# Laying out the rows of three tiles in sixteen shared sections of 1.5 MB, in an instance norm that is bound by DMA

## The chip, the cores and the metric

The kernel runs on one core of a Trainium2 chip. The metric is device time in microseconds of one execution. A ratio in this text is the mean time of one kernel's fast runs over that of the other's fast runs of the same rounds, so it is not quite the ratio of the medians that are quoted beside it.

Some terms: HBM is the memory that holds the input and the output (the page counts 1073.74 MB read from it and as many written), SBUF the memory of the core that holds the tiles, used here as 128 partitions. Sixteen DMA engines copy between them in packets; here a packet is mostly the 64 KB of one partition (32,384 of 37,298 packets in the kernel before). VectorE and ScalarE compute (busy 3298.0 and 2407.7 us there), SyncE issues the copies, and each engine waits for the others by semaphores. The trace has 4144 completions for 259 copies, sixteen for each copy, taken here as one from each DMA engine; a copy has landed with its last completion.

## The reference

```python
# x: (256, 256, 4096) float32, drawn from a normal distribution; eps = 1e-5
mean = np.mean(x, axis=2, keepdims=True)
var = np.var(x, axis=2, keepdims=True)
return ((x - mean) / np.sqrt(var + eps)).astype(np.float32)
```

That is 65,536 independent rows of 16 KB. Each row must be read once and written once, 1073.74 MB each way, and it does not matter which rows are worked on together. The change makes use of that freedom.

## The kernel before

A tile is 512 rows: 128 SBUF partitions with K = 4 adjoining rows each, so one partition's part is 64 KB without a gap. There are 128 tiles of 8 MB and three tile buffers. SyncE issues all loads and stores; VectorE sums the rows and normalizes most of them, ScalarE squares and sums and normalizes the rest.

```python
P, K, BUFS = 128, 4, 3
x_t = x_flat.rearrange("(t p k) d -> t p k d", p=P, k=K)      # tile t, partition p, row k
out_t = out_flat.rearrange("(t p k) d -> t p k d", p=P, k=K)
...
def store(s, t):
    take(S, done[s], K + 1)                    # wait for VectorE and ScalarE
    S.dma_start(out=rows_of(out_t, t), in_=X[s][:, :, :]).then_inc(stored[s], 16)

def load(s, t, wait=True):
    if wait:
        take(S, stored[s], 16)                 # the buffer's last store must have landed
    S.dma_start(out=X[s][:, :, :], in_=rows_of(x_t, t)).then_inc(loaded[s], 16)
...
with S.Fori(0, rounds) as i:                   # the steady state
    for t in range(L0, L0 + BUFS):
        store(t % BUFS, (t, BUFS, rounds, i))
        load((t + 2) % BUFS, (t + 2, BUFS, rounds, i))
```

The first tile is loaded and stored in two halves, and the last one is stored in two. In the built program a load copies from an HBM pattern [128 x 16384] to an SBUF pattern [128 x 16384] (elements of 4 bytes, slowest dimension first).

## Time and profile before

| | before |
|---|---|
| time, median | 4961.8 us (4961.51 to 4986.83) |
| busiest compute engine | VectorE, 66% |
| DMA queue 1, share of 16 engines | 100.0% |
| rate over the span | 433 GB/s |
| pace in steady state | 38.67 us per tile |
| 64 KB packets, median / mean | 2.418 / 2.420 us |

The prediction below shows the page's lines, the waits and the chain. The page's row of rates, one number in GB/s for each fortieth of the span, is this:

```profile
GB/s 422 431 435 433 431 435 433 432 437 432 432 438 432 433 437 432 433 437 432 435 435 432 436 434 431 438 433 431 438 433 432 438 432 433 438 432 433 438 432 405
```

### The profile page before, as it was taken

The page shows a single profiled execution, that of the slowest core. Times are in us where ns is not written, and L with a number is a line of the kernel's source. Part 1 is how long each engine was busy: PE and PEld are TensorE (multiplying, and loading weights), DVE is VectorE, ACT ScalarE, POOL GpSimd, SP SyncE. Part 2 cuts the span into 40 slices and gives each one's busy share as a digit, 9 for nine tenths or more (in the row PEclk, how much of TensorE's full clock was granted, in tenths as well). Part 3 has the DMA queues.
Part 4 walks back from the last instruction along what each step waited for, and adds up shares of the span by engine and source line. Part 5 has one row for each costly group of instructions (what it writes and reads, how often), then busy time and mean ns, then how long its engine had stood idle before and what let it go on. Part 6 is the DMA issues. An engine that isn't in the chain of part 4 may idle for free.

```text
span 4960.2 us, 5938 instructions
## 1 busy us (share of the span) xinstructions
DVE 3298.0 (66%) x2049; ACT 2407.7 (49%) x1412; POOL 0.2 (0%) x4
## 2 busy tenths in 40 slices
DVE  6666666666666666666666666666666666666666
ACT  4455444554445544455445544455444554445544
POOL 0000000000000000000000000000000000000000
DMA  9999999999999999999999999999999999999999
GB/s 422 431 435 433 431 435 433 432 437 432 432 438 432 433 437 432 433 437 432 435 435 432 436 434 431 438 433 431 438 433 432 438 432 433 438 432 433 438 432 405
DMA packets 37298, 2147.52 MB, mean 433 GB/s; under 512 B 4144, under 2 KB 4144, under 8 KB 4144
## 3 DMA queue, kind: packets, MB, share of 16 engines
q1 hardware_dynamic: 37296, 2147.50, 100.0%
q14 instruction: 2, 0.02, 0.0%
HBM read 1073.74 MB, written 1073.74 MB: 433 GB/s over the span
## 4 chain that ended last, share of the span: by engine, by line
DVE 62%; another core or an unknown queue 31%; issue 4%; DMA 2%; ACT 0%; DVEq 0%; ACTq 0%; SPq 0%
DVE x L87 44%; DVE x L112 17%; DMA x<-in_x_dram 1%; DVE nbias L100 1%; DMA out_dram<-x 1%; DVE rstd L98 1%; ACT junk L137 0%; DVEq L68 0%; DVEq L219 0%; ACT L146 0%; ACT std L146 0%; ACTq L68 0%; ACTq L67 0%; SPq L265 0%
## 5 line engine op out<-in xcount | busy, mean ns | idle before, releaser
L87 DVE TENSOR_SCALAR_CACHE_REDUCE x<-x 128x4096 f32<-128x4096 f32 x512 | 2232.3, 4416 | 1580.4 <-DMA x<-in_x_dram 1580.4
L137 ACT ACTIVATE junk<-x,mean 128x4096 f32<-128x4096 f32 x512 | 1883.1, 3678 | 2367.2 <-DVE x L87 2367.2
L112 DVE TENSOR_SCALAR x<-x,rstd,nbias 128x4096 f32<-128x4096 f32 (+1 forms) x512 | 1004.2, 2004 | 33.9 <-DVE nbias L100 29.3
L151 ACT ACTIVATE x<-x,nbias,rstd 128x3072 f32<-128x3072 f32 x130 | 383.2, 2948 | 146.2 <-DVEq L68 146.2
L137 ACT ACTIVATION_READ_ACCUMULATOR junk<-x,mean 128x1 f32 x512 | 95.5, 187 | 0.0
L146 ACT ACTIVATE std<-ss,eps_tile 128x2 f32<-128x2 f32 x256 | 75.6, 295 | 19.1
L98 DVE RECIPROCAL rstd<-std 128x2 f32<-128x2 f32 x256 | 40.7, 159 | 19.4 <-ACT std L146 19.4
L100 DVE SCALAR_TENSOR_TENSOR nbias<-mean,rstd 128x2 f32<-128x2 f32 x256 | 41.1, 161 | 8.9
L87 DVE DVE_READ_ACCUMULATOR x<-x 128x1 f32 x512 | 42.3, 83 | 0.0
L137 ACT ACT_TABLE_LOAD x1 | 1.3, 1283 | 1.2 <-DVE eps_tile L216 1.2
L146 ACT ACT_TABLE_LOAD x1 | 1.3, 1283 | 0.1
L216 DVE MEMSET eps_tile<- 128x1 f32 x1 | 0.1, 59 | 1.0 <-SPq L192 1.0
L251 POOL MEMSET const-bfloat16-1.0<- 128x1 bf16 x1 | 0.1, 101 | 0.0
L251 POOL MEMSET const-uint8-127<- 128x1 uint8 x1 | 0.1, 101 | 0.0
L251 POOL MEMSET const-float32-1.0<- 128x1 f32 x1 | 0.1, 99 | 0.0
L251 POOL MEMSET const-float32-0.0<- 128x1 f32 x1 | 0.1, 98 | 0.2 <-issue 0.2
## 6 DMA issues: line engine op xcount, KB each, us to landing
out_dram<-x SPq DMA_DIRECT2D x4, 4096.0 KB, 19.6
x<-in_x_dram SPq DMA_DIRECT2D x2, 4096.0 KB, 16.7
x<-in_x_dram SPq DMA_DIRECT2D x127, 50.3
out_dram<-x SPq DMA_DIRECT2D x126, 31.5
```

What stands on the lines that cost most here:

```text
L87: V.tensor_scalar(out=x[:, r, :], in0=x[:, r, :], scalar1=1.0 / d, scalar2=None, op0=ALU.mult, op1=ALU.add, accum_out=mean[s][:, r : r + 1 ...
L98: mine(V.reciprocal(out=rstd[s][:, c], in_=std[s][:, c]))
L100: mine(V.scalar_tensor_tensor(out=nbias[s][:, c], in0=mean[s][:, c], scalar=-1.0 / d, in1=rstd[s][:, c], op0=ALU.mult, op1=ALU.mult))
L112: V.tensor_scalar(out=x[:, r, f], in0=x[:, r, f], scalar1=rstd[s][:, c], scalar2=nbias[s][:, c], op0=ALU.mult, op1=ALU.add,).then_inc(dn, 1)
L137: mine(A.activation(out=junk, in_=x[:, r, :], func=AF.Square, bias=mean[s][:, c], scale=-float(d), accum_out=ss[s][:, c]))
L146: A.activation(out=std[s][:, c], in_=ss[s][:, c], func=AF.Sqrt, bias=eps_tile, scale=1.0 / d**3).then_inc(stds, 1)
L151: A.activation(out=x[:, last, :Q], in_=x[:, last, :Q], func=AF.Identity, bias=nbias[s][:, c], scale=rstd[s][:, c]).then_inc(dn, 1)
L216: V.memset(eps_tile, eps / d**2).then_inc(ready, 1)
L251: nc = _bacc.Bacc("TRN2", target_bir_lowering=False, num_devices=1)
```

## The change

The intent is that the DMA engines work farther apart in HBM. Three tiles together take a block of 24 MB, cut into E = 16 sections of 1.5 MB; a tile gets a run of 512 KB (8 partitions) in each section, so its runs lie 1.5 MB apart. The first two tiles stay as they were. Computation, waits and the number of DMAs don't change.

```diff
-    x_t = x_flat.rearrange("(t p k) d -> t p k d", p=P, k=K)
-    out_t = out_flat.rearrange("(t p k) d -> t p k d", p=P, k=K)
     assert ntiles == 128
+    E = 16
+    L0 = ntiles % BUFS
+
+    def by_tiles(ap):
+        groups = ap[L0 * P * K :].rearrange("(i e s j k) d -> s i e j k d", e=E, s=BUFS, k=K, j=P // E)
+        rest = ap[: L0 * P * K].rearrange("(t e j k) d -> t e j k d", e=E, k=K, j=P // E)
+        return groups, rest
+
+    x_t, out_t = by_tiles(x_flat), by_tiles(out_flat)
...
-    def rows_of(ap, t):
-        if isinstance(t, int):
-            return ap[t]
+    def rows_of(tiles, t):
+        groups, rest = tiles
+        if isinstance(t, int):
+            return rest[t] if t < L0 else groups[(t - L0) % BUFS][(t - L0) // BUFS]
         first, period, count, i = t
-        ap = ap[first : first + period * (count - 1) + 1 : period]
-        return ap[bass.ds(i, 1)].rearrange("o p k d -> p (o k) d")
+        assert period == BUFS
+        first -= L0
+        ap = groups[first % BUFS][first // BUFS : first // BUFS + count]
+        return ap[bass.ds(i, 1)].rearrange("o e j k d -> e (o j) k d")
... (the same in the half stores and loads)
```

More of the change, by code (lines that the diff above doesn't have):

```diff
@@ L180, in store_half @@
         take(S, second(done, s, h), half + 1)
-        S.dma_start(out=out_t[t][:, r, :], in_=X[s][:, r, :]).then_inc(second(stored, s, h), 16)
+        S.dma_start(out=rows_of(out_t, t)[:, :, r, :], in_=X[s][:, r, :]).then_inc(second(stored, s, h), 16)
     def halves(tile_fn, s, first):
@@ L189 @@
     rounds = (ntiles - 5) // BUFS
-    L0 = 2
     with tc.tile_critical():
@@ L194 @@
             r = half_of(h)
-            S.dma_start(out=X[0][:, r, :], in_=x_t[0][:, r, :]).then_inc(second(loaded, 0, h), 16)
+            S.dma_start(out=X[0][:, r, :], in_=rows_of(x_t, 0)[:, :, r, :]).then_inc(second(loaded, 0, h), 16)
         load(1, 1, wait=False)
```

## The prediction

> **What bounds the kernel now.** I read the page's busy shares and slices first, then its DMA part, then the table of waits, then the chain of work in the middle of the run, and last the records of single DMA packets in the trace.
>
> ```profile
> DVE 3298.0 (66%) x2049; ACT 2407.7 (49%) x1412; POOL 0.2 (0%) x4
> ...
> DMA  9999999999999999999999999999999999999999
> ...
> DMA packets 37298, 2147.52 MB, mean 433 GB/s; under 512 B 4144, under 2 KB 4144, under 8 KB 4144
> ...
> q1 hardware_dynamic: 37296, 2147.50, 100.0%
> HBM read 1073.74 MB, written 1073.74 MB: 433 GB/s over the span
> ```
>
> No compute engine is over 66% busy; the DMA row is 9 in all forty slices, and the packets of queue 1 fill 100.0% of the time of sixteen engines. The bytes are the least possible (1073.74 MB read once, written once). So the time is bytes divided by the rate of the DMA engines.
>
> ```profile
> DVE x L87 <- DMA x<-in_x_dram: 1580.4, 126, 13.2
> ...
> SPq L68 <- DVE x L112: 4757.1, 130, 38.3
> ```
>
> The columns are total us, number of waits, longest. VectorE waits 126 times for a load, 1580.4 / 126 = 12.5 us each: that is its slack in every tile. SyncE's wait for VectorE is long because it issues early and then has nothing to do, not because the DMA rings are empty.
>
> ```profile
> 2009.18 12.44 another core or an unknown queue
> ...
> 2021.72 17.45 DVE x L87 x8
> ...
> 2047.80 12.49 another core or an unknown queue
> ...
> 2060.39 17.45 DVE x L87 x8
> ```
>
> This is the chain of work in steady state; the columns are start and length in us. The row named "another core or an unknown queue" is the wait for a load. One tile takes 2060.39 - 2021.72 = 38.67 us, in which 16.78 MB move: 434 GB/s.
>
> The packet records say the same of one engine: of 32,384 packets of 64 KB (one partition's four rows) the median is 2.418 us, 27.1 GB/s, and the mean 2.420. All bytes at the median would take 32,768 x 2.418 / 16 = 4952.1 us. The span is 4960.2, so 8.1 us in all are above that, start and end included. Only 373 packets took over 2.43 us, 66.4 us too much between them, or 4.1 us per engine.
>
> [...]
>
> **The change part by part.** Compute: VectorE, ScalarE and SyncE have the same instructions in the same order, the same waits and the same number of DMAs (259). Cost 0. Bytes and packets: a partition still holds four adjoining rows, 64 KB, so there should again be 32,384 packets of 64 KB. Cost 0. The first two tiles keep their places.
>
> Addresses in HBM: neighbouring runs of a tile lie 1.5 MB apart instead of side by side. At best all 373 slow packets go: -4.1 us. The early tiles, with the most of them, are unchanged in part, so I count -2.
>
> Shape: this is what the intent does not mention. The HBM side was [128 x 16384] and is now [16 x 8 x 16384], for 126 loads and 126 stores; the SBUF side stays 128 partitions.[...]
>
> [...]Four rows are 4 x 2.418 = 9.67 us. [...]The slack of 12.5 us per tile allows such a lead.
>
> [...]126 tiles cost another 126 x 38.67 = 4872 us: about 9830.[...]
>
> What in the trace speaks for a quick settling is that engines already drift apart in before. The sixteen completions of a load land within 0.4 us at 13 us, 2.4 us at 220 us, 5.1 us at 570 us, and 7.4 us from 1150 us on. The number of slow packets falls with it, from 51 in the first fortieth of the span to 3 to 6 in those around the middle. [...]one-sided and soon over, a loss of about one full lead.
>
> Sum: 4961.8 - 2 + 9.7 + 3 (the last store ends with its last engine, spread 6.5 us in before, now perhaps 9.7) = 4972.5 us.
>
> **Rivals.** First, nothing happens[...]. For it: the author's intent leaves it out[...]. Time: 4958 to 4963. Second, [...]For it: [...]ten of the sixteen completions still lie within 0.8 us of each other at the end of before[...]. Time: 6000 to 9830. Third, slow settling[...]: 5060 to 6000. Fourth, a gain from HBM spacing:[...] a gain over 2% needs packets under 2.37 us, of which before has none.
>
> **Range and chances.** I give nothing-happens and quick settling 0.58 together, slow settling 0.14, lasting collisions 0.27, faster by over 2% 0.01. The predicted time is that of the likeliest case, 4972 us. The lower end is the floor of 4952.1 less a margin, 4948. The upper end cuts off most of the lasting collisions: 7000.
>
> **What would show it.** The packet part should again have 37,298 packets and 2147.52 MB; more packets would mean that rows were cut, and my account of the shape is wrong. [...]many 64 KB packets take up to 4.8 us, first slices of the GB/s row fall to half, and VectorE's wait for loads grows from 12.5 us. Quick settling shows as one or two low slices and then 433; lasting collisions as an even low row.[...] A span under 4948 would make the whole account wrong.

## More of the kernel before

All runs here have a granted clock of 1.0.

One more view is useful for later, the timeline around the first load of tile 2; its columns are start, length, engine, line, operation, and in brackets the idle time before.

```profile
48.78 0.46 SPq L170 DMA_DIRECT2D x<-in_x_dram  x1
...
82.51 4.42 DVE L87 TENSOR_SCALAR_CACHE_REDUCE x<-x 128x4096 f32<-128x4096 f32 x1 [8.22 <-DMA x<-in_x_dram]
```

The load is issued at 48.78 us, queues behind a store whose last completion comes at 63.26 us, and VectorE can start on it at 82.51 us.

## The result

The changed kernel takes 9084.94 us (median of 4 runs, 9007.18 to 9097.58) against 4961.8 us: a ratio of 1.8265, 95% interval 1.8162 to 1.8369. The result is correct. The predicted 4972 us and the range of 4948 to 7000 us were wrong.

First the page of the changed kernel, the lines that answer to those in the prediction. The row GB/s has one number for each fortieth of the span.

```profile
DVE 3298.2 (37%) x2049; ACT 2407.6 (27%) x1412; POOL 0.2 (0%) x4
...
DMA  9999999999999999999999999999999999999998
GB/s 292 250 245 241 239 238 241 236 237 236 237 238 237 237 235 238 235 238 236 236 236 239 240 238 238 237 238 239 238 235 237 238 237 235 235 234 236 237 236 212
DMA packets 37298, 2147.52 MB, mean 238 GB/s; under 512 B 4144, under 2 KB 4144, under 8 KB 4144
...
q1 hardware_dynamic: 37296, 2147.50, 99.6%
HBM read 1073.74 MB, written 1073.74 MB: 238 GB/s over the span
```

VectorE does the same work in the same 3298 us. The packets and bytes are the same to the last one. The DMA engines are busy in every slice, as before; but they move 238 GB/s in place of 433. A row of nines says that packets are under way, not that they are fast. The GB/s row below it shows the loss: low from the start and even to the end.

Now the waits of VectorE in the changed kernel (total us, times, longest), and in a second fence those of SyncE.

```profile
DVE x L96 <- DMA x<-in_x_dram: 5582.0, 127, 48.4
```

```profile
SPq L77 <- DVE x L121: 8019.1, 129, 66.3
SPq L77 <- DMA out_dram<-x: 777.0, 126, 70.6
```

VectorE waits 44.0 us for each load in place of 12.5. SyncE waits longer for the same things, and for stores too (777.0 us, which was 47.7 before). No new kind of wait ends the chain, whose steady state is this (start and length in us):

```profile
4012.29 44.03 another core or an unknown queue
...
4056.42 17.45 DVE x L96 x8
...
4082.50 46.00 another core or an unknown queue
...
4128.60 17.45 DVE x L96 x8
```

A tile takes 4128.60 - 4056.42 = 72.18 us, 1.87 times the 38.67 of before. VectorE's 17.45 us for the four sums are unchanged.

The most telling place is the first load of the new form. This is the timeline of the changed kernel there, then a table of three stretches of it (length, then busy time of the engines, clock, DMA share and GB/s).

```profile
48.81 0.69 SPq L182 DMA_DIRECT2D x<-in_x_dram  x1
...
103.36 4.42 DVE L96 TENSOR_SCALAR_CACHE_REDUCE x<-x 128x4096 f32<-128x4096 f32 x1 [29.03 <-DMA x<-in_x_dram]
```

```profile
24.00:60.00 36.00, 27.26 (x17) 24.02 (x14) 0.00 (x0) 1.00 1.01 421
62.00:104.00 42.00, 12.68 (x11) 10.29 (x6) 0.00 (x0) 1.00 0.99 218
...
4000.00:6000.00 2000.00, 734.12 (x458) 535.07 (x314) 0.00 (x0) 1.00 1.00 238
```

It is issued at the same time as before (48.81 us) but VectorE starts on it at 103.36 us, 20.9 us later. Up to 60 us, with the old form, the rate is 421 GB/s; in the stretch of this load it is 218. That stretch takes in the ends of the copies beside it: the load's own 8.39 MB took 40 us, from 63 to 103 us, which is 209 GB/s, or 48% of the 434 GB/s of the steady state before. The trace's records of single packets say how it was slow:

```
64 KB packets       number under 2.43 us   number over 4.5 us   mean us
before                     32011                     0           2.420
changed                     2431                 21811           4.398
changed, those started between 80 and 100 us:
                               0              64 of 64            5.06
completions of that load on the sixteen engines: 102.5 to 103.2 us
```

These packets take 2.09 times as long as in before, a little more than double, and all sixteen engines finish within 0.7 us of one another. No engine won and none lost. This already contradicts the step of the prediction that counted on one-sided collisions.

### The profile page after: what moved, and what is told of

The parts are those of the page before. It is cut to its first block, busy times and chain, and to the rows that moved or that the text cites. A ratio compares the mean times of both kernels' runs of the same rounds, so it can differ in the third digit from the quotient of the medians.

```text
span 9005.4 us, 5938 instructions
## 1 busy us (share of the span) xinstructions
DVE 3298.2 (37%) x2049; ACT 2407.6 (27%) x1412; POOL 0.2 (0%) x4
## 2 busy tenths in 40 slices
DMA packets 37298, 2147.52 MB, mean 238 GB/s; under 512 B 4144, under 2 KB 4144, under 8 KB 4144
## 3 DMA queue, kind: packets, MB, share of 16 engines
q1 hardware_dynamic: 37296, 2147.50, 99.6%
## 4 chain that ended last, share of the span: by engine, by line
another core or an unknown queue 62%; DVE 35%; issue 2%; ACT 0%; DMA 0%; DVEq 0%; ACTq 0%; SPq 0%
DVE x L96 25%; DVE x L121 9%; DVE nbias L109 1%; DVE rstd L107 0%; ACT junk L146 0%; DMA x<-in_x_dram 0%; DVEq L77 0%; DVEq L230 0%; ACT std L155 0%; ACT L155 0%; ACTq L77 0%; ACTq L76 0%; SPq L276 0%; SPq L203 0%
## 6 DMA issues: line engine op xcount, KB each, us to landing
x<-in_x_dram SPq DMA_DIRECT2D x127, 108.9
```

## The experiments

The theory after the result: in the new shape, DMA engines that are at work at the same moment slow one another down, below called a collision (5.06 us for a packet in place of 2.418), all of them alike, and go on doing so. What they would collide on is not shown, as no record names what an engine uses. Rivals: the new HBM addresses are slow in themselves (spacing of the engines, or interleaving of tiles); or computation and waits add to it. The kernel before, run beside each of them, always had a median between 4961.7 and 4962.3 us, with single runs up to 5007.96.

### x1: contiguous tiles again, but the HBM side stays [16 x 8]

```diff
-        groups = ap[L0 * P * K :].rearrange("(i e s j k) d -> s i e j k d", ...)
+        groups = ap[L0 * P * K :].rearrange("(i s j e k) d -> s i e j k d", ...)
```

> HBM side [16 x 8 x 16384] as in the changed kernel, but each tile is one 8 MB block again, runs 64 KB apart[...]. Theory[...]: as slow as the changed kernel, 8800 to 9300 us, 64 KB packets mostly near 5 us. Rival (HBM addresses: runs 1.5 MB apart collide in HBM): about 4962 us, packets at 2.418 us.

Measured: 9083.55 us (9027.86 and 9139.24), ratio 1.8306. The rate by fortieths of the span in this run:

```profile
GB/s 290 248 238 236 236 236 237 234 234 236 234 232 234 233 234 234 233 234 233 232 234 233 233 234 233 233 233 233 234 233 233 232 233 234 234 232 232 234 234 213
```

This is the same curve as the changed kernel's, without any 1.5 MB in it and with every tile one block of 8 MB as before (the steps are 64 KB from run to run and 1 MB inside a run). So the 1.5 MB between runs is not needed for the slowdown; the shape is enough.

### x2: 32 runs in place of 16

```diff
-    E = 16
+    E = 32
```

> Three tiles still share 24 MB, but in 32 runs of 768 KB (4 partitions each) in place of 16 of 1.5 MB. Theory: the HBM side's slowest dimension is now 32[...]: 4955 to 4970 us, packets at 2.418 us.[...] Rival (HBM addresses or interleaved tiles): clearly slow, 7000 us or more.

Measured: 4990.65 us (4962.43 to 5011.47), ratio 1.0044 (0.9998 to 1.0089). Three tiles still share 24 MB. One number in the source, and the loss is gone. The page of this run again has 37,298 packets; its mean 64 KB packet is 2.438 us, and its rate stays up to the end:

```profile
GB/s 422 433 434 434 434 431 432 435 435 433 431 435 434 429 432 428 427 430 428 428 428 428 433 429 428 428 428 429 428 428 429 431 431 429 428 428 429 433 428 394
```

Why 16 runs are slow and 32 are not is not shown: no record says which partitions an engine has.

### x3: 128 runs

```diff
-    E = 16
+    E = 128
```

> Three tiles share 24 MB in 128 runs, one partition per run, 192 KB apart; both sides of the copy have 128 as slowest dimension, as in the kernel before. Theory: [...]4955 to 4970 us, packets at 2.418 us. Rival (interleaving tiles in HBM costs rate): slower than 5100 us.

Measured: 4980.91 us (4962.97 to 5007.28), ratio 1.0056 (1.0015 to 1.0097); mean packet 2.420 us. Interleaving the tiles in HBM costs nothing that shows beside the spread that before has too.

### x4: only the loads in the new form

Stores go to contiguous tiles, so the rows come out permuted and the result is wrong.

```diff
-    x_t, out_t = by_tiles(x_flat), by_tiles(out_flat)
+    x_t, out_t = by_tiles(x_flat), in_order(out_flat)   # in_order: "(i s e j k) d -> s i e j k d"
```

> Wrong result on purpose (rows land permuted): loads as in the changed kernel, stores as in the kernel before. Theory: only the loads (writes into SBUF) collide, half of the extra: 4962 + (9085 - 4962)/2 = about 7020 us, loads slow and stores at 2.418 us per packet.[...] Rival (HBM reads at 1.5 MB pitch): cannot be told apart here from the theory; x1 to x3 do that.

Measured: 7504.41 us (7455.16 and 7553.67), ratio 1.5124. In the profiled run 14,019 packets of 64 KB took under 2.43 us and 14,175 over 4.5 us; 126 tiles have 16,128 packets in each direction. Linked in the order of time, each packet to one that starts where it ends, they come in eights: about eight at 2.42, then about eight near 4.9. The loads collide nearly all the time: 126 x 19.34 us, a second time for each load, would be 2437 us, and the two runs took 2493 and 2592 more than 4962, which is over it because a slow packet takes more than double (5.06 us in the first load). So the loads bear more than half of the 4123 us; I had expected half.

### x5 and x11: only the stores in the new form

```diff
-    x_t, out_t = by_tiles(x_flat), by_tiles(out_flat)
+    x_t, out_t = in_order(x_flat), by_tiles(out_flat)
```

> Wrong result on purpose: the mirror of x4_loads_only, loads as in the kernel before and stores as in the changed kernel. Theory: only the stores (reads of SBUF) collide. x4 took 2542 us more than before of the 4123 that the changed kernel takes more, so what is left for the stores is 4123 - 2542 = 1581: about 6540 us if the two add up; if alone they collide as fully as loads, 7400 to 7500. Rival ([...]stores suffer from sharing with loads): about 4970 us.

> x5 again with more rounds, as its two runs were 6269 and 6699 us. Theory: one steady mechanism, 6200 to 6800 us[...]. Rival (x5 fell into a slow state): back near 4970 us.

Measured: 6269.24 and 6698.69 us, then 6443.56 to 6866.25 us. Most of these runs count as slow because they are over 1.5% above the fastest of their kernel, at the same clock of 1.0. The two that count as fast, 6269.24 and 6443.56 us, are 1307 and 1482 us above before. So stores suffer by themselves, less than loads and less evenly. Fast loads and fast stores-only runs add up to 3800 to 4074 us, near the 4123 of the whole change; but the other stores-only runs lie up to 1904 us above before, so the sum proves little. Why stores vary more stays open.

### x6: a quarter of the computation

Wrong result; the control for the runs below.

```diff
# in vector_tile and scalar_tile, for every wide instruction:
-    x[:, r, :]   ...   slice(0, d)   ...   junk   ...   x[:, last, :Q]
+    x[:, r, :1024] ... slice(0, 1024) ... junk[:, :1024] ... x[:, last, :1024]
```

> Wrong result on purpose: the changed kernel with every compute instruction cut to 1024 of 4096 columns; all DMAs as they are. Control for x7. Theory: the time is set by the DMA engines, so 8900 to 9200 us. Rival (VectorE or the waits on it add to the changed kernel's time): clearly under 8500 us.

Measured: 9010.34 us (8947.87 and 9072.81), ratio 1.8132. VectorE is busy 12% of the span in this run, and the time is the changed kernel's. Computation has no part in it that shows.

### x7: twelve of the sixteen engines start behind, four of them twice as far

x6, with two copies from HBM to an unused HBM tensor, of four and of twelve rows, before the first load of the new form. A row is four packets of 64 KB here, 4 x 2.418 = 9.67 us. The plan was that each row holds up one engine for that long, and that the second copy reaches the four engines of the first again; the rival, that the order of the engines in time makes no difference. The page has 16 packets under 512 B more than that of x6 (4160 and 4144), as many as there are rows. No record names an engine; how many engines were late, and by how much, is seen in the completions.

```diff
+    AHEAD = 4
+        for at, engines in ((0, 4), (4, 12)):
+            S.dma_start(out=unused[at : at + engines, : AHEAD * K * d], in_=apart[at : at + engines]).then_inc(held, 16)
         load(2, 2, wait=False)
```

> Wrong result on purpose: x6_light with two unused copies put before the first [16 x 8] load[...]. The small compute leaves slack for it. Theory ([...]a lead is kept): back to 4980 to 5300 us, most packets at 2.418 us. Rival 1 (the lead is not kept[...]): starts fast and ends at 9000, total 6000 to 9000. Rival 2[...]: about 9000 us from the start.

Measured: 5078.84 us (5069.42 and 5088.25), ratio 1.022 to before (1.0146 to 1.0294, unclear at 2%), against 9010 for x6. These are the stretches of x7 (the last column is GB/s):

```profile
70.00:200.00 130.00, 23.60 (x47) 19.10 (x33) 0.00 (x0) 1.00 1.00 413
200.00:1000.00 800.00, 166.87 (x322) 134.72 (x221) 0.00 (x0) 1.00 1.00 432
1000.00:3000.00 2000.00, 430.02 (x832) 347.44 (x572) 0.00 (x0) 1.00 1.00 432
3000.00:5000.00 2000.00, 422.97 (x817) 342.72 (x563) 0.00 (x0) 1.00 1.00 422
```

The shape, the addresses and every later DMA are those of x6; only the order in time of the engines differs (and the two copies are added), and the full rate is back, and holds for nearly the whole run. Of 32,448 packets of 64 KB, 29,084 took under 2.43 us and 214 over 4.5 us. The completions of the first load came in three groups of four, eight and four engines, at 89.2 to 89.6, 98.8 to 100.2 and 108.9 to 109.6 us, near the steps of 9.67 us that had been planned. So it matters which engines are at work at the same moment.

### x12: a stagger of the same size between two groups of eight

```diff
-        for at, engines in ((0, 4), (4, 12)):
+        for at, engines in ((0, 8),):
```

> Wrong result on purpose: x7 with one unused copy[...]. Theory[...]: no help, 8900 to 9150 us like x6. Rival (any staggering of the engines, in HBM for instance, is what brought x7 back): 4980 to 5500 us.

Measured: 8894.12 and 9068.29 us (the second counts as slow). Eight engines were a whole 11 us behind the other eight (completions of the first load at 102.9 to 103.9 and at 114.6 to 114.9 us), and it helped next to nothing (9010.34 us without it, in x6). This rules out that any stagger would do. x7 had three groups apart, of four, eight and four engines, and ran at 425 GB/s over its span; x12 had two groups of eight apart, and ran at 242. So setting those two groups of eight apart leaves the collisions; which engine collides with which is not shown.

### x9: half the stagger

```diff
-    AHEAD = 4
+    AHEAD = 2
```

> Wrong result on purpose: x7 with 2 packets in place of 4 in each unused copy[...]. Theory (a lead is kept[...]): a tile takes 1.5 times as long, 4962 + 126 x 19.3 = about 7400 us, half-way between x7 and x6, and steady over the run. Rival 1 (collisions are one-sided and widen the lead): settles at full speed, 5100 to 5400 us. Rival 2 (a partial lead is lost again): drifts to the pace of x6, 8500 to 9000 us.

Measured: 9019.99 us (9000.63 and 9039.36), ratio 1.8177. None of the three expectations holds as written; rival 2 is the nearest. The rate by fortieths of the span (225 us each):

```profile
GB/s 333 260 245 239 236 235 236 235 235 236 235 236 237 236 237 236 235 235 236 237 237 235 237 235 236 237 239 239 241 239 237 235 237 238 237 235 237 236 236 203
```

It starts better and has lost everything within three slices. The completions of the first loads show how:

```
completions in us (number of engines), x9
first load        100.9-102.1 (4)   111.1-112.4 (8)   114.2-114.7 (4)
fourth landing    164.3-166.7 (4)   182.6-183.0 (4)   189.0-200.8 (8)
eighth landing    276.6 (1)         286.2-289.4 (10)  298.2-327.8 (5)
```

The three groups were planned two packets, 2 x 2.418 = 4.84 us, apart. The lead of the first four over the next eight had grown to a full block of four packets (about 10 us, 101 to 111 us), while that of the eight over the last four had shrunk to about 3 us (111 to 114 us). At the fourth landing four engines are 16 us or more ahead of the twelve others. Whoever was ahead then came to the end of what was issued, and had to wait for the next DMA, which SyncE issues only after the slowest engine's part of an earlier one. So it was here: the store that is the eighth landing was issued at 247.50 us, after the slowest part of an earlier load had landed at 238.0 us, and eight engines had by then finished the seventh (231.7 to 246.0 us). At the eighth landing ten engines finish within 3.2 us of one another: they have been brought abreast. So a lead is not simply kept, as I had assumed, and in this place the completion waits took it away from those who had it. Why the smaller lead shrank in the first load rather than staying as it was is not settled.

### x10: the whole stagger with the whole computation

The copies of x7 in the changed kernel itself; the result is right.

> Right result: the changed kernel with its full compute and the two unused copies of x7 (four packets). [...]the four groups of engines start 0, 9.67, 9.67 and 19.3 us late, while the slack of a tile with full compute is 12.5 us. Theory: the foremost group is held by the waits for VectorE and loses about 7 us of its lead[...]: 7000 to 8500 us. Rival (the waits do not cut a lead): about 5000 us as x7.

Measured: 9064.93 us (9026.85 and 9103.01), ratio 1.8267, slower than the 7000 to 8500 expected.

```profile
GB/s 355 234 237 240 235 237 234 234 233 238 235 236 234 234 237 238 238 238 237 236 241 238 237 235 235 237 239 235 236 234 234 236 239 234 236 233 233 237 236 212
```

The first load comes in with groups at 90, 100 and 109.6 us, as in x7, and from 70 to 200 us the rate is 345 GB/s. Then the foremost group, 19.3 us ahead with a slack of 12.5, is held: its completions go from 128.5 to 129.1 us to 159.1 to 161.0 us, some 31 us for a transfer of 19.3. The store that it waits for was issued only at 136.62 us, when VectorE had worked on the load whose last part landed at 109.7 us. From the second slice on the rate is that of the changed kernel. The direction was as expected, the size not, since what remains of a lead is lost as in x9. A lead that fits in 12.5 us for all engines was not tried: the four engines of the first copy were again among the twelve of the second, as the groups of four, eight and four show.

### x8: 1.5 MB between runs, with 32 runs as in x2

Six tiles share 48 MB in 32 runs of four partitions, 1.5 MB from run to run.

```diff
-    E = 16
+    E = 32
+    SHARE = 6      # in place of BUFS in by_tiles, rows_of and the loops: 20 rounds of six, three tiles after them
```

> [...]six tiles share 48 MB in 32 runs of 256 KB (four partitions), 1.5 MB from run to run[...]. Theory: 4955 to 4990 us, same as before[...]. Rival (1.5 MB spacing costs or gains in HBM): outside 4940 to 5060 us.

Measured: 4962.55 us (4962.31 to 4962.85), ratio 0.9986 (0.9932 to 1.004). The page's lines for this run:

```profile
DMA  9999999999999999999999999999999999999999
GB/s 422 431 435 432 432 435 433 435 434 433 436 432 433 436 433 432 436 433 434 435 433 436 433 433 437 432 433 436 433 433 436 432 436 434 432 436 433 433 437 399
```

This is what the change was meant to do, and it does nothing: the mean packet is 2.420 us, as in before. No version here beats the kernel before.

## Why the prediction was wrong

**The bound: right.** DMA engines at 2.418 us per 64 KB packet set the time, and the changed kernel (mean packet 4.398 us) and x6 (9010.34 us with a quarter of the computation) show that they still do.

**Compute, packets and bytes at no cost: right.** VectorE is busy 3298.2 us in place of 3298.0, with 37,298 packets and 2147.52 MB in both. (The 126 stores of the prediction are 125 whole ones and two halves; nothing hangs on it, and its other sums come out as written.)

**HBM spacing, -2 us: no gain seen.** x8 has the spacing without the collisions and a mean packet of 2.420 us, and 378 packets over 2.43 us where before had 373. An effect of 2 us is below what these runs resolve.

**The shape: right that it can slow the copies.** x1 shows that the shape alone is enough (9083.55 us with runs 64 KB apart, 9084.94 with 1.5 MB), x2, x3 and x8 that interleaved tiles and 1.5 MB between runs alone do nothing (ratios 1.0044, 1.0056 and 0.9986), x7 and x12 that it matters which engines are at work together (5078.84 and 8894.12 us). The records do not name an engine or anything that engines share, so what the collisions are on is not shown; that the shape would bring them was the author's estimate. In the first load of the new form a slow packet took 5.06 us, a little over the 4.8 that the prediction named.

**The failed step: "one-sided and soon over, a loss of about one full lead."** A full lead is four packets, 4 x 2.418 = 9.67 us. In its place the runs showed an even slowing: the first load of the new form took 40 us on all sixteen engines, with completions 0.7 us apart. The loss was not one lead of 9.7 us but 4123 us, 85% of the 126 x 38.67 = 4872 us that a second time for every tile would be. The evidence was misread: the drift in the kernel before, 0.4 to 7.4 us between the completions of a load, is among engines of which none had a packet over 4.5 us, so it said nothing about how engines fare that slow one another to 5.06 us. There was no figure on that in the profile, so nothing in it spoke for the one-sided case over an even one. Why it is even stays open.

**The expectation for a partial lead: wrong too.** x9 was to be half as bad, at 7400 us, and took 9019.99; its lead of 4.84 us was not kept. **The slack of 12.5 us "allows such a lead": too simple.** x10 shows the foremost group, 19.3 us ahead, held to 31 us for a transfer of 19.3, and x9 shows ten engines brought to within 3.2 us of one another after the completion waits. So the tile-wise waits took a lead away in both, which I had not considered.

**The rivals.** "Lasting collisions", at 6000 to 9830 us, was the one that came true. It had 0.27 of the chances, and the upper end of the range cut it off.

## What to carry to other kernels

When an access pattern is reshaped, measure its copies anew, even if the packets, the bytes and the busy share of the engines stay: with 128 partitions in SBUF, an outermost HBM dimension of 16 made this kernel 1.83 times as long, and 32 or 128 left it as it was (1.0044 and 1.0056). A DMA row full of nines is no proof of a full rate (99.6% busy at 238 GB/s here, 100.0% at 433 before); look at GB/s and at the time of one packet. And look at the packets before reordering addresses: with nearly all of them at 2.418 us in before, none of the three other orders that kept this packet time (x2, x3, x8) gained anything.
